# The down projections of a two-layer encoder: eleven Strassen pairs instead of ten pairs and two plain chunks, with the order of all queues written out

## The chip, the cores and the metric

One core of a Trainium2 chip runs the whole program in one launch. The metric is device time in microseconds (us) of one execution; less is better. The time before is the median of three runs.

## What is computed

The program is a bidirectional encoder trunk on 512 tokens of width 1024, two layers. Each layer has a half-step SwiGLU feed-forward block, an attention mixer, a second half-step feed-forward block and a gated per-layer input; a final RMSNorm closes it. All in float32. The part that matters here is the feed-forward block, run four times:

```python
def rmsnorm(x, g):
    y = xf * lax.rsqrt(jnp.mean(xf * xf, axis=-1, keepdims=True) + RMS_EPS)
    return (y * g.astype(jnp.float32)).astype(x.dtype)

def swiglu(x, w_gate, w_up, w_down):
    return (jax.nn.silu(x @ w_gate) * (x @ w_up)) @ w_down
...
for i in range(DEPTH):
    h = h + 0.5 * swiglu(rmsnorm(h, norm_ffn1[i]), ffn1_w_gate[i], ffn1_w_up[i], ffn1_w_down[i])
    ...
    h = h + 0.5 * swiglu(rmsnorm(h, norm_ffn2[i]), ffn2_w_gate[i], ffn2_w_up[i], ffn2_w_down[i])
    gate = jax.nn.sigmoid(rmsnorm(h, norm_ple[i]) @ w_ple_gate[i])
    h = h + gate * (p[i] @ w_ple_proj[i])
```

The inner width is 2816, that is 22 chunks of 128.

## The kernel before, in words

**Splitting.** Every float32 product is made of three TensorE matmuls on operands cut in two: a high part (ScalarE copies the value to the float32r type, L153) and a low part (VectorE subtracts the high part from the value, L154). `split` (L152) does both; `mm` runs high x high, high x low, low x high into the same PSUM bank. Weights come in tiles `wr` of 128x1024 (`WR` = 5 buffers) or `tmp` of 128x512 (`TMPS` = 10); their parts lie in `wh` and `wl` (4 buffers each).

**A feed-forward block** (`ffn`, L454). `front` and five calls of `block` make the gate and up products. Their rows are turned back by TensorE transposes (`turn_back`, L443: four transposes into a PSUM bank, then a ScalarE copy out at L450) into chunks `a[0..21]`, each 128 inner features x 512 tokens. `between` turns one block's rows while the next block runs; the last block's four chunks are turned inside the down stage, by the function `turn`. `inner_sums` (L492) makes three VectorE sums per pair of chunks, for pairs whose chunks are there (`READY`).

**The down stage** (`down`, L501) multiplies the chunks by the down weights. Two chunks (`WHOLE` = 2) are multiplied plainly: `rx`, then the halves `left` and `right`. The other 20 form `K2` = 10 pairs, each a 2x2 block product in Strassen's form (Winograd's variant), seven products of halves instead of eight. The functions `first` to `seventh` are these products; each takes a unit of two pairs, so there are five units. A product of one unit is 12 matmuls of 128x128 by 128x512: two pairs, two banks, three parts (L542 to L544).

The seven products need weights b11, b21, b22, b11 + b12 and so on. The sums of weights are made in the buffer itself: GpSimd issues a DMA that adds the next block to what lies there (`add`, L533) once the present weights have been split. `first` (L572) loads b11 (`load`, L517) and adds b12, which `fifth` uses; `summed` (L562) loads b12 and b22 and adds them on VectorE (L567), which `seventh` uses; adding b11 gives the weights of `sixth`, adding b21 those of `fourth`. `second` and `third` load b21 and b22 into `tmp` tiles through `halved` (L526).

**What sets the order.** The loops in `down` only state the work. The scheduler of the framework orders each engine's queue, by priorities in program order and its own estimate of when things are ready; buffers of the pools add the waits. Each engine runs its queue in that order and waits in place for what an instruction needs. SP's queue issues the loads, GpSimd's the adding loads. `tc.keep_in_program_order` (L150, in `put`) fixes the place of single instructions; before, only the setup uses it.

After the last product of a stage, the four output quarters are transposed (L677), added to the residual rows `hs`, which are loaded from DRAM (`kept`), and normed for the next stage, whose first matmuls are L178 to L180 or L803 to L805.

## Time and profile before

| | |
|---|---|
| median of 3 runs | 2003.8 us (2002.4 to 2007.15) |
| the profiled execution | 2005.77 us |
| its span, first to last instruction | 2003.9 us |
| mean granted TensorE clock | 0.997 |
| down stages in it, from the first to the last matmul | 230 to 343, 859 to 972, 1252 to 1364, 1817 to 1933 us |
| DMA over the span | 173 GB/s |

A row of the timeline has start, length, engine, line and operation, the tile written and those read, the shape, and in brackets the idle time before it and what ended it. PE is TensorE's matmul, PEld its weight load, DVE VectorE, ACT ScalarE, POOL GpSimd; a q behind the name is that engine's queue of issues. In a table of windows each engine's busy time stands with its number of instructions, and behind them the granted clock (1.00 is full), the share of the DMA engines and GB/s.

### The profile page before, as it was taken

The page shows a single profiled execution, that of the slowest core. Times are in us where ns is not written, and L with a number is a line of the kernel's source. Part 1 is how long each engine was busy: PE and PEld are TensorE (multiplying, and loading weights), DVE is VectorE, ACT ScalarE, POOL GpSimd, SP SyncE. Part 2 cuts the span into 40 slices and gives each one's busy share as a digit, 9 for nine tenths or more (in the row PEclk, how much of TensorE's full clock was granted, in tenths as well). Part 3 has the DMA queues.
Part 4 walks back from the last instruction along what each step waited for, and adds up shares of the span by engine and source line. Part 5 has one row for each costly group of instructions (what it writes and reads, how often), then busy time and mean ns, then how long its engine had stood idle before and what let it go on. Part 6 is the DMA issues. An engine that isn't in the chain of part 4 may idle for free.

```text
span 2003.9 us, 28013 instructions
## 1 busy us (share of the span) xinstructions
PE 1976.0 (99%) x9726; PEld 1646.1 (82%) x9726; DVE 1537.0 (77%) x2648; ACT 1213.0 (61%) x2051; POOL 324.7 (16%) x378
## 2 busy tenths in 40 slices
PE   9999999999999999999999999999999999999997
PEld 7888788879888888878888888788888888887886
DVE  7787897798767677797786778877888668778775
ACT  7656765477645565675566556745766556666553
POOL 1111011341211221111122110011000122110111
PEclk9999999999999999999999999999999999999999
DMA  9877687543426787878568786785343577776961
GB/s 274 196 198 174 170 213 225 141 95 78 96 73 221 173 184 173 195 188 222 189 214 186 178 190 168 209 212 162 104 129 100 188 181 188 176 173 177 230 222 43
DMA packets 151069, 346.12 MB, mean 173 GB/s; under 512 B 26384, under 2 KB 34064, under 8 KB 150928
## 3 DMA queue, kind: packets, MB, share of 16 engines
q1 hardware_dynamic: 112704, 236.28, 36.0%
q0 software_dynamic: 38080, 108.02, 30.5%
q8 instruction: 76, 1.25, 0.2%
q14 instruction: 65, 0.53, 0.1%
q10 hardware_dynamic: 144, 0.04, 0.0%
HBM read 315.96 MB, written 17.27 MB: 166 GB/s over the span
## 4 chain that ended last, share of the span: by engine, by line
PE 87%; DVE 5%; DMA 3%; issue 3%; ACT 2%; POOL 0%; DVEq 0%; ACTq 0%; POOLq 0%
PE mm L368 7%; PE mm L369 7%; PE mm L367 7%; PE mm L178 5%; PE mm L180 5%; PE mm L179 5%; PE sc L367 3%; PE sc L369 3%; PE sc L368 3%; PE mm L544 3%; PE mm L542 3%; PE mm L543 3%; PE sc L543 2%; PE sc L544 2%; PE sc L542 2%
## 5 line engine op out<-in xcount | busy, mean ns | idle before, releaser
L153 ACT ACTIVATE wh<-wr 128x1024 fp32r<-128x1024 f32 (+1 forms) x408 | 427.2, 1050 | 424.2 <-DMA wr<-in_gu_dram 82.3
L154 DVE TENSOR_TENSOR wl<-wr,wh 128x1024 fp32r<-128x1024 f32 (+1 forms) x408 | 496.2, 1219 | 199.5 <-ACT wh L153 197.0
L367 PE MATMUL mm<-wh,act 128*128 128x512 f32 x640 | 250.9, 392 | 0.0
L369 PE MATMUL mm<-wh,act 128*128 128x512 f32 x640 | 250.7, 392 | 0.0
L368 PE MATMUL mm<-wl,act 128*128 128x512 f32 x640 | 249.5, 390 | 0.6 <-DVE wl L154 0.5
L153 ACT ACTIVATE wh<-tmp 128x512 fp32r<-128x512 f32 x264 | 155.6, 625 | 95.8 <-PE sc L369 32.6
L178 PE MATMUL mm<-act,wh 128*128 128x512 f32 (+1 forms) x472 | 184.8, 393 | 0.4 <-ACT act L153 0.4
L179 PE MATMUL mm<-act,wh 128*128 128x512 f32 (+1 forms) x472 | 184.5, 391 | 0.0
L180 PE MATMUL mm<-act,wl 128*128 128x512 f32 (+1 forms) x472 | 184.4, 391 | 0.0
L154 DVE TENSOR_TENSOR wl<-tmp,wh 128x512 fp32r<-128x512 f32 x264 | 171.5, 683 | 4.1 <-ACT wh L153 3.7
L337 POOL DMA_DIRECT2D wr<-in_gu_dram x80 | 80.4, 1020 | 379.8 <-DVE wl L154 360.6
L368 PEld LDWEIGHTS mm<-wl,act 128*128 128x128 f32 x640 | 120.2, 188 | 25.7 <-DVE wl L154 1.5
L369 PEld LDWEIGHTS mm<-wh,act 128*128 128x128 f32 x640 | 120.2, 188 | 24.4
L367 PEld LDWEIGHTS mm<-wh,act 128*128 128x128 f32 x640 | 120.3, 188 | 23.8
L154 DVE TENSOR_TENSOR act<-act,act 128x512 fp32r<-128x512 f32 (+1 forms) x216 | 133.8, 634 | 3.8 <-ACT act L153 3.7
L153 ACT ACTIVATE act<-act 128x512 fp32r<-128x512 f32 (+1 forms) x216 | 120.7, 582 | 24.0 <-DVE act L311 9.9
L367 PE MATMUL sc<-wh,act 128*128 128x512 f32 x320 | 124.6, 389 | 1.6 <-DVE act L291 1.6
L369 PE MATMUL sc<-wh,act 128*128 128x512 f32 x320 | 124.7, 390 | 0.0
L368 PE MATMUL sc<-wl,act 128*128 128x512 f32 x320 | 124.5, 389 | 0.0
L409 DVE TENSOR_TENSOR wr<-wr,wr 128x1024 f32<-128x1024 f32 x40 | 49.0, 1225 | 87.8 <-DMA wr<-in_gu_dram 87.6
L533 POOL DMA_DIRECT2D wr<-in_dn_dram x60 | 51.9, 864 | 365.9 <-DVE wl L154 325.3
L345 POOL DMA_DIRECT2D tmp<-in_gu_dram x80 | 74.8, 1200 | 221.8 <-DVE act L498 137.0
(272 smaller groups left out, 4631.3 us busy)
## 6 DMA issues: line engine op xcount, KB each, us to landing
wr<-in_gu_dram SPq DMA_DIRECT2D x92, 512.0 KB, 5.2
tmp<-in_gu_dram SPq DMA_DIRECT2D x160, 256.0 KB, 3.7
wr<-in_gu_dram POOLq DMA_DIRECT2D x80, 512.0 KB, 7.6
tmp<-in_dn_dram SPq DMA_DIRECT2D x144, 256.0 KB, 4.0
wr<-in_dn_dram POOLq DMA_DIRECT2D x60, 512.0 KB, 6.3
tmp<-in_gu_dram POOLq DMA_DIRECT2D x80, 256.0 KB, 5.9
wr<-in_dn_dram SPq DMA_DIRECT2D x40, 512.0 KB, 4.4
act<-kept SPq DMA_DIRECT2D x56, 256.0 KB, 4.5
```

The lines of the kernel that those rows point to most:

```text
L153: self.put(self.nc.scalar.activation(hi, src, AF.Copy))
L154: self.put((lo_eng or self.nc.vector).tensor_tensor(lo, src, hi.bitcast(F32), op=ALU.subtract))
L178: mm(out, stat[0], mov[0], start=start, stop=False)
L179: mm(out, stat[0], mov[1], start=False, stop=False)
L180: return mm(out, stat[1], mov[0], start=False, stop=stop)
L337: nc.gpsimd.dma_start(raw, q[:, u * UNIT:(u + 1) * UNIT], accum_op=ALU.add)
L367: mm(p, xh, wh, start=start and k == 0, stop=False, skip_group_check=True)
L368: mm(p, xh, wl, start=False, stop=False, skip_group_check=True)
L369: self.last_mm = mm(p, xl, wh, start=False, stop=stop and k == half - 1, skip_group_check=True)
L542: mm(p, xh, wh, start=start and k == 0, stop=False, skip_group_check=True)
L543: mm(p, xh, wl, start=False, stop=False, skip_group_check=True)
L544: ins = mm(p, xl, wh, start=False, stop=stop and k == u.stop - 1, skip_group_check=True)
```

## The change

All 22 chunks now form pairs: `K2` = 11, `WHOLE` and all that served it are gone, and the weights are laid out in four quarters of eleven blocks (`_quarters`). The eleven pairs make six units, the first of one pair, the others of two. `READY` is 9, so that nine pairs have their inner sums before the stage.

A list `order` says in which order the 42 products run. Product by product, three functions are called: `product` (the matmuls), `after` (what follows certain products: transposes, copies out of banks, closing sums, loads of the residual) and `ahead`, which calls `prepare` (splits, sums, adding loads) for the product `LEAD` + 1 = 4 places on and `load` for the one 7 places on (3 and 6 before the first product runs). While `pinned` is set, `put` keeps all these instructions in program order on TensorE, VectorE, ScalarE, GpSimd and SP.

In a product the three parts now run one behind the other over the whole unit (high x high for both pairs and banks, then low operand x high weight, then high operand x low weight). The operand splits of the b halves are made as halves of 128x256 just ahead of `second` and `fourth`, not whole. The transposes of the last block's chunks use the `tr` banks, not the `sc` banks, and run in two groups, behind `first` of unit 2 and `fifth` of unit 1.

```diff
-WHOLE = 2
-READY = 8
-K2 = (NF - WHOLE) // 2
+READY = 9
+K2 = NF // 2
+LEAD = 3
+LOADS = 6
...
-                self.nc.tensor.transpose(p[:, b * P:(b + 1) * P], x[:, c * P:(c + 1) * P], self.ident)
-            self.nc.scalar.activation(a, p, AF.Copy)
+                self.put(self.nc.tensor.transpose(p[:, b * P:(b + 1) * P], x[:, c * P:(c + 1) * P], self.ident))
+            self.put(self.nc.scalar.activation(a, p, AF.Copy))
...
+        units = [range(1)] + [range(u, u + 2) for u in range(1, K2, 2)]
...
+        def half_split(x):
+            t = self.act(F32R)
+            self.split(x, t[:, l], t[:, r])
+            return t[:, l], t[:, r]
+
+        def inner_split(s):
+            for k in units[s]:
+                x3[k] = self.split_chunk(sums[k], nc.vector)
+                put(tt(B[k][:, l], B[k][:, l], sums[k][:, r], op=ALU.add))
...
+        def load(kind, s):
+            u = units[s]
+            if kind == "first":
+                raws[s] = wide(b11, u)
+            elif kind == "seventh":
+                raws[n + s], more[s] = wide(b12, u), narrow(b22, u)
+            elif kind in ("second", "third"):
+                more[kind, s] = narrow(b21 if kind == "second" else b22, u)
...
+        def prepare(kind, s):
+            u = units[s]
+            if kind == "first":
+                w = self.parts(raws[s])
+                add(raws[s], b12, u)
+                for k in u:
+                    if sums[k] is None:
+                        sums[k] = self.inner_sums(A[k], B[k])
+                    x1[k] = self.split_chunk(A[k], nc.vector)
+                x = x1
+            elif kind == "second":
+                w, x = halved(more.pop((kind, s))), {k: half_split(B[k][:, l]) for k in u}
+            elif kind == "fifth":
+                w, x = self.parts(raws.pop(s)), x1
+            elif kind == "seventh":
+                for j, y in enumerate(more.pop(s)):
+                    z = raws[n + s][:, j * T:(j + 1) * T]
+                    put(tt(z, z, y, op=ALU.add))
+                w, x = self.parts(raws[n + s]), x3
+                add(raws[n + s], b11, u)
+                if u.start not in x3:
+                    inner_split(s)
+            elif kind == "sixth":
+                w, x = self.parts(raws[n + s]), x3
+                add(raws[n + s], b21, u)
+            elif kind == "fourth":
+                for k in u:
+                    x2[k] = half_split(B[k][:, r])
+                w, x = self.parts(raws.pop(n + s)), x2
+            else:
+                for k in u:
+                    x4[k] = half_split(B[k][:, l])
+                w, x = halved(more.pop((kind, s))), x4
+            ops[kind, s] = w, x
+            if kind == "fifth" and 0 < s < 4:
+                inner_split(s - 1)
...
+            for a, b in ((0, 0), (1, 0), (0, 1)):
+                for j, k in enumerate(u):
+                    for i, p in enumerate(out):
+                        c = slice(cols.start + i * P, cols.start + (i + 1) * P)
+                        put(nc.tensor.matmul(p, x[k][a][:, c], w[b][:, j * T:(j + 1) * T], start=start and k == a == b == 0,
+                                             stop=stop and b == 1 and k == u.stop - 1, skip_group_check=True))
...
+        order = [(k, s) for s in range(n - 1) for k, s in (("second", s), ("first", s), ("fifth", s - 1)) if s >= 0]
+        order += [("seventh", 0), ("second", 5), ("first", 5), ("fifth", 4), ("seventh", 1), ("sixth", 0), ("seventh", 2),
...
+            elif (kind, s) == ("fourth", 0) and inner:
+                self.p = inner()
...
+        ahead(LEAD)
+        for i, step in enumerate(order):
+            product(*step)
+            if step == ("fourth", 5):
+                ahead(i + LEAD + 1)
+                after(*step)
+            else:
+                after(*step)
+                ahead(i + LEAD + 1)
```

The list goes on with seventh 2, fifth 5, sixth 1, seventh 3, fourth 0, sixth 2, third 0, seventh 4, fourth 1, sixth 3, seventh 5, fourth 2, sixth 4, fourth 3, sixth 5, fourth 4, third 1, fourth 5, and then third 2 to 5 (the number is the unit). The number of TensorE matmuls outside the down stages and their order do not change.

Three places show the moves. First VectorE's queue in the first down stage of the kernel before, where the first b12 + b22 sum (L567, tile `wr_530`) stands among operand splits (L154 writing `act`) and a weight split (L154 writing `wl`).

```order
L594 TENSOR_TENSOR act_253_1203<-act_253_1203,act_255_1213 128x256
L496 TENSOR_TENSOR act_466_2281<-act_466_2281,act_468_2288 128x256
L567 TENSOR_TENSOR wr_530_2533<-wr_530_2533,tmp_531_2535 128x512
L154 TENSOR_TENSOR act_475_2303<-act_313_1526,act_474_2302 128x512
L154 TENSOR_TENSOR wl_496_2384<-wr_490_2373,wh_495_2383 128x1024
L154 TENSOR_TENSOR act_477_2307<-act_317_1540,act_476_2306 128x512
```

Now the same sum (L566, tile `wr_501`) stands behind the splits of `first` and `fifth` of the units that run before it, directly ahead of the split of its own weights; its unit is the one of a single pair.

```order
L155 TENSOR_TENSOR act_506_2414<-act_380_1874,act_505_2413 128x512
L155 TENSOR_TENSOR act_508_2418<-act_384_1888,act_507_2417 128x512
L155 TENSOR_TENSOR wl_512_2438<-wr_463_2240,wh_511_2437 128x1024
L155 TENSOR_TENSOR act_514_2442<-act_255_1213,act_513_2441 128x512
L516 TENSOR_TENSOR act_250_1193<-act_250_1193,act_255_1213 128x256
L155 TENSOR_TENSOR act_516_2447<-act_256_1217,act_515_2446 128x512
L516 TENSOR_TENSOR act_254_1207<-act_254_1207,act_256_1217 128x256
L566 TENSOR_TENSOR wr_501_2392<-wr_501_2392,tmp_502_2394 128x512
L155 TENSOR_TENSOR wl_519_2467<-wr_501_2392,wh_518_2466 128x512
L155 TENSOR_TENSOR wl_521_2484<-tmp_509_2421,wh_520_2483 128x512
```

The sum has moved from the head of operand splits to their end. Second, SP's queue of loads before, around the load of that sum's weights (L517, `wr_530`); L566 are the b22 blocks of this and later sums, L526 weights of `second`.

```order
L526 DMA tmp_541_2570<-in_dn1_dram 128x512
L526 DMA tmp_542_2571<-in_dn1_dram 128x512
L566 DMA tmp_544_2592<-in_dn1_dram 128x512
L566 DMA tmp_545_2595<-in_dn1_dram 128x512
L517 DMA wr_530_2533<-in_dn1_dram 128x1024
L566 DMA tmp_553_2650<-in_dn1_dram 128x512
L566 DMA tmp_554_2653<-in_dn1_dram 128x512
```

Now the load (L520, `wr_501`) stands with its own b22 block (`tmp_502`) ahead of the loads of `second` (`tmp_509`, `tmp_510`) and `first` of unit 5 (`wr_517`).

```order
L520 DMA wr_480_2310<-in_dn1_dram 128x1024
L520 DMA wr_501_2392<-in_dn1_dram 128x512
L526 DMA tmp_502_2394<-in_dn1_dram 128x512
L526 DMA tmp_509_2421<-in_dn1_dram 128x512
L526 DMA tmp_510_2422<-in_dn1_dram 128x512
L520 DMA wr_517_2451<-in_dn1_dram 128x1024
L520 DMA wr_524_2495<-in_dn1_dram 128x1024
```

Each product's loads now stand together, in the order of the products. Third, VectorE's queue now, at the preparation of `seventh` of unit 4 in the same stage: two sums (L566), the low weight part, the two inner splits with their sums (L516), then the operands of `fourth` of unit 1.

```order
L566 TENSOR_TENSOR wr_567_2696<-wr_567_2696,tmp_568_2698 128x512
L566 TENSOR_TENSOR wr_567_2696<-wr_567_2696,tmp_569_2699 128x512
L155 TENSOR_TENSOR wl_578_2757<-wr_567_2696,wh_577_2756 128x1024
L155 TENSOR_TENSOR act_580_2762<-act_387_1901,act_579_2761 128x512
L516 TENSOR_TENSOR act_382_1881<-act_382_1881,act_387_1901 128x256
L155 TENSOR_TENSOR act_582_2767<-act_388_1905,act_581_2766 128x512
L516 TENSOR_TENSOR act_386_1895<-act_386_1895,act_388_1905 128x256
L155 TENSOR_TENSOR act_586_2783<-act_184_849,act_586_2783 128x256
```

Nothing of another product stands between the sums and the split that needs them.

More of the change, by code (lines that the diff above doesn't have):

```diff
@@ L409, in fifth @@
                 tt(base[i], base[i], chain[i], op=ALU.add)
-            late()
             product(A, base, t12, r, False, False)
@@ L499, in inner_sums, with down @@
         return s
-    def down(self, w, a, xs, x1, sums, begin, kept, inner, turn):
+    def down(self, w, a, sums, kept, inner, turn):
         nc, H = self.nc, T // 2
@@ new lines, in product @@
+        def product(kind, s):
+            u, (w, x) = units[s], ops.pop((kind, s))
+            out = {"first": r1, "second": r2, "fifth": r3, "seventh": rb, "sixth": r1, "fourth": rc, "third": r3}[kind]
+            cols = r if kind in ("fifth", "sixth") else l
+            start, stop = kind not in ("sixth", "third"), s == n - 1
+            for a, b in ((0, 0), (1, 0), (0, 1)):
[4 more added lines that the diff above has]
+                                             stop=stop and b == 1 and k == u.stop - 1, skip_group_check=True))
@@ L562, in summed @@
-        def summed(s):
-            raws[s] = load(b12, units[s])
-            for j, k in enumerate(units[s]):
-                x, more = raws[s][:, j * T:(j + 1) * T], self.tmp()
-                nc.sync.dma_start(more, b22[:, k * T:(k + 1) * T])
-                tt(x, x, more, op=ALU.add)
-        def first(s):
-            u = units[s]
-            raw = raws[s] = load(b11, u)
-            for k in u:
-                if sums[k] is None:
-                    with self.tc.issue_after(marks[s - 2].ins):
-                        sums[k] = self.inner_sums(A[k], B[k])
-                x1[k] = x1[k] or self.split_chunk(A[k], nc.vector)
-            marks.append(product(r1, u, self.parts(raw), x1, l, True, last(u)))
-            add(raw, b12, u)
@@ L598, in sixth @@
-        def sixth(s):
-            u = units[s]
-            product(r1, u, self.parts(raws[s]), x3, r, False, last(u))
-            add(raws[s], b21, u)
-        def fourth(s):
-            u = units[s]
-            product(rc, u, self.parts(raws[s]), x2, r, False, last(u))
-            for k in u:
-                t = self.act(F32R)
-                x4[k] = t[:, l], t[:, r]
-                self.split(B[k][:, l], *x4[k])
-        for s in range(n):
-            first(s)
-            if s == 1:
-                turn(range(2))
-            second(s)
-            if s == 1:
-                turn(range(2, 4))
-                r3 = [self.sbank(), self.sbank()]
-                c5 = copied(rx)
-            if s > 1:
-                fifth(s - 2)
@@ new lines, in down, with ahead @@
+        for i, step in enumerate(order[:LOADS]):
+            load(*step)
+            if i < LEAD:
+                prepare(*step)
+        self.pinned, end = True, len(order)
+        def ahead(i):
+            if i < end:
+                prepare(*order[i])
+            if i + LOADS - LEAD < end:
+                load(*order[i + LOADS - LEAD])
+        ahead(LEAD)
[4 more added lines that the diff above has]
+                after(*step)
+            else:
+                after(*step)
+                ahead(i + LEAD + 1)
```

191 lines of the change are left out of this document (67 added, 124 removed).

## The prediction

> **What bounds the kernel now.** I read the page first, then the waits of TensorE, then the timeline of the down stages.
>
> ```profile
> PE 1976.0 (99%) x9726; PEld 1646.1 (82%) x9726; DVE 1537.0 (77%) x2648; ACT 1213.0 (61%) x2051; POOL 324.7 (16%) x378
> PEclk9999999999999999999999999999999999999999
> ```
>
> TensorE is busy for 99% of the span at full granted clock, so time goes only by fewer matmuls or fewer gaps between them. The waits of TensorE (us in total, times, longest) name where it stands still:
>
> ```profile
> PE mm L544 <- DVE act L154: 4.7, 4, 2.1
> PE sc L449 <- ACT act L450: 3.2, 4, 0.8
> ```
>
> Both rows stand in the down stages, four times each, once per stage: 4.7 + 3.2 = 7.9 us.
>
> How fast it goes between gaps comes from the first down stage's timeline: its first matmul, two that bracket an undisturbed run, and its last.
>
> ```profile
> 230.03 0.39 PE L542 MATMUL tr<-wh,act 128*128 128x512 f32 x1
> ...
> 256.13 0.39 PE L542 MATMUL mm<-wh,act 128*128 128x512 f32 x1
> ...
> 272.22 0.39 PE L544 MATMUL sc<-wh,act 128*128 128x512 f32 x1
> ...
> 343.08 0.40 PE L544 MATMUL sc<-wh,act 128*128 128x512 f32 x1
> ```
>
> From 256.13 to 272.22 there are 71 starts: 16.09 / 71 = 0.2266 us a matmul. (The 0.39 is the pipelined length, not the pace.) How many there are, from the groups by line (L542 is one of the three matmuls of a split product, L543 and L544 have equal counts):
>
> ```profile
> L542 PE MATMUL mm<-wh,act 128*128 128x512 f32 x256 | 100.4, 392 | 0.0
> L542 PE MATMUL sc<-wh,act 128*128 128x512 f32 x176 | 69.3, 394 | 0.0
> L542 PE MATMUL ob<-wh,act 128*128 128x512 f32 x96 | 37.6, 392 | 0.0
> L542 PE MATMUL tr<-wh,act 128*128 128x512 f32 x96 | 37.4, 389 | 0.0
> ```
>
> 256 + 176 + 96 + 96 = 624, times 3 is 1872, 468 per down stage. First and last matmul of the other three stages:
>
> ```profile
> 859.12 0.39 PE L542 MATMUL tr<-wh,act 128*128 128x512 f32 x1
> ...
> 972.30 0.40 PE L544 MATMUL sc<-wh,act 128*128 128x512 f32 x1
> ...
> 1251.72 0.39 PE L542 MATMUL tr<-wh,act 128*128 128x512 f32 x1
> ...
> 1364.48 0.40 PE L544 MATMUL sc<-wh,act 128*128 128x512 f32 x1
> ...
> 1817.21 0.39 PE L542 MATMUL tr<-wh,act 128*128 128x512 f32 x1
> ...
> 1932.93 0.40 PE L544 MATMUL sc<-wh,act 128*128 128x512 f32 x1
> ```
>
> From first to last start the four stages take 113.05, 113.18, 112.76 and 115.72 us; 468 matmuls alone are 106.05. With the last matmul's own 0.23 the first stage has 113.28 - 106.05 = 7.2 us that are not matmuls; 40 transposes lie in it.
>
> **Where it stands still.** TensorE's rows around the two waits in the first stage:
>
> ```profile
> 240.91 1.04 PE L449 MATMUL sc<-ident,act 128*128 128x128 f32 x8
> ...
> 242.76 1.14 PE L449 MATMUL sc<-ident,act 128*128 128x128 f32 x8 [0.81 <-ACT act L450]
> ...
> 243.76 0.50 PE L542 MATMUL mm<-wh,act 128*128 128x512 f32 x1
> ...
> 248.18 0.39 PE L542 MATMUL sc<-wh,act 128*128 128x512 f32 x1
> ...
> 249.51 0.74 PE L544 MATMUL mm<-wh,act 128*128 128x512 f32 x2 [0.94 <-DVE act L154]
> ```
>
> The second group of eight transposes takes 1.00 us (242.76 to 243.76), 0.125 each; the first took 1.85, so 0.85 us went on waiting for ScalarE's copy out of the two banks. From 248.18 to 249.51 are 1.33 us instead of 0.23: 1.10 lost, waiting on VectorE for the low part of an operand. What VectorE was doing, and the load it waited for on SP's queue:
>
> ```profile
> 243.50 0.33 SPq L517 DMA_DIRECT2D wr<-in_dn_dram  x1
> ...
> 248.16 0.69 DVE L567 TENSOR_TENSOR wr<-wr,tmp 128x512 f32<-128x512 f32 x1 [2.12 <-DMA wr<-in_dn_dram]
> 248.77 0.69 DVE L154 TENSOR_TENSOR act<-act,act 128x512 fp32r<-128x512 f32 x1
> ```
>
> The load of the b12 weights was issued at 243.50. VectorE stood 2.12 us at the sum that needs it, and the operand split behind it in its queue (248.77) is the one TensorE wanted. So it is a load issued too late, met by an instruction queued too early. With transposes at 0.11 to 0.125 us each, 40 of them take 4.4 to 5.0 of the 7.2 us, so the stage's standstill, short restarts behind the waits among it, is 2.2 to 2.8 us; I take 2.3. In the fourth stage the same wait is longer, 2.11 us, and is followed by slow starts:
>
> ```profile
> 1837.87 0.73 PE L544 MATMUL mm<-wh,act 128*128 128x512 f32 x2 [2.11 <-DVE act L154]
> ...
> 1839.13 0.57 PE L543 MATMUL mm<-wl,act 128*128 128x512 f32 x1
> ...
> 1842.48 0.45 PE L544 MATMUL mm<-wh,act 128*128 128x512 f32 x1
> ```
>
> ```profile
> 1837.00:1841.00 4.00, 3.13 (x10) 2.50 (x11) 4.00 (x7) 0.00 (x0) 0.86 (x1) 0.77 0.33 76
> ```
>
> Between 1839.13 and 1842.48 eight matmuls take 3.35 us, not 1.81: 1.5 us more, at a mean granted clock of 0.77. The Trainium skill ("TensorE: Matmul & The Clock Gate", section "Why this matters for your kernels") asks only that idle gaps stay under about 3 us; by it this gap would have cost itself alone and the removable time would be 1.5 us less. Here a gap of 2.11 us was enough, so the measurement decides: a new wait above about 2 us is priced at itself plus 1.5.
>
> By the lengths of the stages (0.13 more, 0.29 less and 2.67 more than the first), the four lose 2.3 + 2.4 + 2.0 + 5.0 = 11.7 us; 13.7 with transposes at 0.11.
>
> **The change part by part.** *Eleven pairs by seven products.* Two of the 22 chunks went through the plain product: 2 chunks x 4 quarter products x 2 banks x 3 = 48 matmuls, beside 10 x 42 = 420. Now 11 x 42 = 462. Six fewer per stage, 24 in all, at 0.2266: 5.4 us, directly on TensorE's path, since nothing else is left to cover.
>
> *One written order.* The load of the first b12 unit now stands on SP's queue ahead of three products' worth of other loads, and the sum that needs it stands on VectorE's queue behind the operands of all products that run before it (the order rows above). That removes the wait for VectorE in every stage (4.7 us in the list) and the fourth stage's slow clock. The transposes of the last block now come in two groups with a product of 12 matmuls (2.7 us) between, which is longer than the wait of 0.85, so it goes too. Gone in the best case: all 11.7 us (13.7).
>
> *What is late next: VectorE.* Its load in the first down stage, in the order sum, TensorE, weight loads, VectorE, ScalarE, GpSimd:
>
> ```profile
> 230.00:361.00 131.00, 129.25 (x613) 107.06 (x612) 106.30 (x167) 77.49 (x121) 16.46 (x22) 1.00 0.80 214
> ```
>
> VectorE is at 106 of 131 us. The change adds to it per stage about 23 splits of 128x256 and one 128x512 weight split, one b12 sum and one set of pair sums, and takes ten 128x512 operand splits and two closing sums away. Its pace per operation by start-to-start distances, and one weight activation of ScalarE:
>
> ```profile
> 232.04 1.41 DVE L440 SCALAR_TENSOR_TENSOR act<-act,minus,act 128x512 f32<-128x512 f32 x2
> ...
> 236.91 0.68 DVE L154 TENSOR_TENSOR wl<-tmp,wh 128x512 fp32r<-128x512 f32 x1
> 237.51 1.22 DVE L154 TENSOR_TENSOR wl<-wr,wh 128x1024 fp32r<-128x1024 f32 x1
> 238.64 0.41 DVE L594 TENSOR_TENSOR act<-act,act 128x256 f32<-128x256 f32 x1
> ...
> 244.95 0.75 DVE L594 TENSOR_TENSOR act<-act,act 128x256 f32<-128x256 f32 x2
> ```
>
> ```profile
> 235.71 1.06 ACT L153 ACTIVATE wh<-wr 128x1024 fp32r<-128x1024 f32 x1 [0.52 <-ACT act L153]
> ```
>
> 128x512: 0.60 (236.91 to 237.51); 128x1024: 1.13 (237.51 to 238.64); 128x256: about 0.34 (a second one adds 0.33 to the 0.42 of a first). So 23 + 4 (of the sums) at 0.34, less 12 - 2 at 0.60: 9.2 - 6.0 = +3.2 us, about 109 of 129. On average it is covered. Locally, per product of 12 matmuls (2.72 us of TensorE): second and third 1.9 us, first 2.3, fifth and sixth 1.1, fourth 1.8, seventh 5.3 when it also splits its inner sums (two sums 1.2; then a standstill of 1.06 until ScalarE has made the high part; the low part 1.13; 2 x (0.60 + 0.34)). The four weight buffers let a product's preparation begin when the product three before it starts. For the seventh of unit 4 that is "fourth" of unit 0 (6 matmuls), "sixth" of 2 (12), "third" of 0 (6): 5.44 us against 5.3. For the seventh of unit 5: three products, 8.16 us, against 1.8 + 1.1 + 5.3 = 8.2. So both come in with nothing to spare; where the stage also splits two per-layer inputs (second and fourth stage), 1.2 us more falls into the second of these. In its favour, the new matmul order takes the high-by-high third first, so the operand's low part is wanted 0.9 us and the weight's 1.8 us after the product starts. At the start of a stage, VectorE's last two gate/up products (232.04, done at 233.45, 3.4 us into the stage) stand ahead of the two operand splits of the second "first" (1.2 us), so that these end at 4.6, while its turn comes after 6 + 6 + 12 matmuls, at 5.4: close, but early enough.
>
> I take 1.0 us per stage for all this, between 0 and the 2.1 us of the longest wait the trace has in these stages: 4 us in all, ends 0 and 8.4.
>
> *Loads.* Quarter blocks read per stage: 88 instead of 86 of 256 KB, +2.3%, no term. An accumulating load, issued by GpSimd when the first split of its buffer is done, lands as follows (median of issues by line; then min, median, max of L533):
>
> ```profile
> wr<-in_dn_dram POOLq DMA_DIRECT2D x60, 512.0 KB, 6.3
> ```
>
> ```profile
> DMA to landing us min/median/max: 5.3/6.3/9.3
> ```
>
> The closest users are now three products, 8.16 us, apart, as they were; at 6.3 us that is covered, at 9.3 not (third rival).
>
> *Tail, gate/up.* The end of a stage has the same transposes and evictions; one more set of pair sums in gate/up, 1.0 us of VectorE, lies under TensorE work. Zero for both; if the tail's cover is gone, a 1 us wait per stage, inside the range.
>
> **Sum.** 5.4 + 11.7 - 4.0 = 13.1 us. The profiled execution took 2005.8 us (span 2003.9, 1.9 around it), so 1992.7; the median of the three runs is 2.0 lower, 2003.8, so 1990.7, and I say 1990.5.
>
> **Rivals.** *Half the gain.* The sevenths' chain on VectorE costs 2 to 3 us a stage, since its two inner waits (sum, ScalarE, split) can no longer be filled by other work in a fixed order. For it: the margins of 0.1 us above, and a wait over 2 us brings the slow clock. Against it: low parts are wanted late. Gain 5.4 + 11.7 = 17.1 less 8 to 13: 4 to 9 us, 1995 to 1999.5.
>
> *Nothing.* Removed waits are replaced by equal ones: a gain within 4 us, 2000 to 2007.
>
> *Slower: the accumulating loads hold the fixed queues.* ScalarE already waits for them, by the waits of the first stage's window:
>
> ```profile
> ACT wh L153 <- DMA wr<-in_dn_dram: 19.3, 7, 4.2
> ```
>
> Seven waits, up to 4.2 us; now every later preparation stands behind such a wait. Place: seventh, sixth and fourth of unit 5, which hand one buffer on through two landings. The low weight part of that seventh is done 1.9 us before its product may start (the inner splits come behind it), and 7 products of 2.72 lie between the starts of seventh and fourth: 20.9 us for two landings and two splits of 1.06 + 1.13, so 8.2 us a landing. At the median 6.3 nothing waits. At 9.3, the maximum seen, 2.1 us are lost, with the slow clock 3.6 a stage, 14.4 of the 17.1 us of gain. At 10.5 it is 4.6 + 1.5 = 6.1 a stage, 24.4 in all, so 2003.8 + 7.3 = 2011. It decides from about 10 us on; only the maximum speaks for it. The Trainium skill (same page, Part 1) calls the queues of VectorE and ScalarE strictly first in, first out, which is the mechanism of this rival; the trace agrees (VectorE's 2.12 us at the b12 sum held the split behind it).
>
> That the order isn't what is written is excluded by the rows of the order.
>
> **Numbers.** Forecast (10 to 19 us gained) 0.6, half the gain 0.2, nothing 0.1, slower 0.1. The range reaches from 2003.8 - 5.4 - 13.7 = 1984.7, rounded down, to the top of the half gain, 1999.5, and leaves out the last two. About 0.2%, 4 us, is what a measurement of this kernel can tell from no change: faster 0.8, same 0.1, slower 0.1.
>
> **What would show it.** Right: 1848 matmuls of the down stages at 0.227 us; the waits on VectorE's low part and on ScalarE's copy in the list of TensorE's waits gone; stage lengths near 109 to 111 us each; no granted clock below 1 in the fourth. Half: TensorE waiting on VectorE or ScalarE ahead of a seventh or the product behind it. Slower: ScalarE waiting for accumulating loads with TensorE behind it, at the fourths and sixths of the last units. The prediction is wrong if the stages shrink by less than the 1.4 us that six matmuls are worth.

## The result and the profile after

The changed kernel takes 2024.27 us (median of four runs, 2023.78 to 2025.72), the kernel before beside it 2004.31: a ratio of 1.010 (95% interval 1.0082 to 1.0117), 20.0 us slower, where 13.3 us faster was forecast. The profiled execution took 2024.63 us, its span is 2022.8 us (+18.9) and its mean granted clock 0.992 (0.997 before). Medians here are of the runs at the usual clock: one run each of experiments 4 and 9, at a mean granted clock of 0.75 and 0.85, doesn't count.

The page after, and the waits of TensorE:

```profile
PE 1981.2 (98%) x9702; PEld 1649.2 (82%) x9702; DVE 1551.9 (77%) x2716; ACT 1217.7 (60%) x2107; POOL 335.2 (17%) x390
```

```profile
PE tr L614 <- DVE act L630: 12.5, 6, 3.0
PE mm L595 <- ACT wh L154: 9.3, 5, 5.3
```

The 24 matmuls are gone (9726 to 9702), and so are both old waits. Two new ones stand in their place, 21.8 us in all. L614 are the transposes of the tail, L630 the evictions of `second_half`, L595 the matmuls of the products, L154 ScalarE's high parts. First and last rows of the four stages, from the timeline of TensorE:

```profile
229.63 0.39 PE L595 MATMUL mm<-wh,act 128*128 128x512 f32 x1
...
347.02 1.08 PE L595 MATMUL sc<-wl,act 128*128 128x512 f32 x4
...
864.27 0.39 PE L595 MATMUL mm<-wh,act 128*128 128x512 f32 x1
...
986.25 1.07 PE L595 MATMUL sc<-wl,act 128*128 128x512 f32 x4
...
1266.18 0.39 PE L595 MATMUL mm<-wh,act 128*128 128x512 f32 x1
...
1379.32 1.08 PE L595 MATMUL sc<-wl,act 128*128 128x512 f32 x4
...
1831.87 0.39 PE L595 MATMUL mm<-wh,act 128*128 128x512 f32 x1
...
1951.66 1.08 PE L595 MATMUL sc<-wl,act 128*128 128x512 f32 x4
```

With three more starts in each last row (0.68 us), the stages take 118.1, 122.7, 113.8 and 120.5 us, 475.0 in all, against 454.7: +20.3 us. The rest of the program is 1.4 us shorter. All of the loss is in the down stages, most of it at two places.

**The tail, in every stage.** TensorE at the end of the first stage:

```profile
331.81 2.09 PE L595 MATMUL sc<-wh,act 128*128 128x512 f32 x8
333.74 1.08 PE L595 MATMUL sc<-wl,act 128*128 128x512 f32 x4
337.75 2.15 PE L614 MATMUL tr<-ident,act 128*128 128x128 f32 x8 [2.94 <-DVE act L630]
339.56 3.76 PE L595 MATMUL sc<-wh,act 128*128 128x512 f32 x8
343.12 1.34 PE L595 MATMUL sc<-wl,act 128*128 128x512 f32 x4
```

Behind third 3 eight transposes want the two `tr` banks, 2.94 us before VectorE has emptied them; the eight matmuls after it take 3.56 us (339.56 to 343.12), where those of third 3 took 1.93 (331.81 to 333.74). VectorE in the same stretch, and ScalarE's two rows that hold it up:

```profile
318.42 1.23 DVE L155 TENSOR_TENSOR wl<-wr,wh 128x1024 fp32r<-128x1024 f32 x1 [2.53 <-ACT wh L154]
...
324.62 1.23 DVE L155 TENSOR_TENSOR wl<-wr,wh 128x1024 fp32r<-128x1024 f32 x1 [2.44 <-ACT wh L154]
325.77 1.28 DVE L656 TENSOR_TENSOR act<-act,tr 128x512 f32<-128x512 f32 x2
...
328.17 0.75 DVE L155 TENSOR_TENSOR act<-act,act 128x256 fp32r<-128x256 f32 x2
...
334.47 1.28 DVE L155 TENSOR_TENSOR wl<-tmp,wh 128x512 fp32r<-128x512 f32 x2
335.67 0.68 DVE L662 TENSOR_TENSOR act<-mm,act 128x512 f32<-128x512 f32 x1
...
336.87 1.07 DVE L630 SCALAR_TENSOR_TENSOR act<-tr,act 128x256 f32<-128x256 f32 x3
```

```profile
317.32 1.06 ACT L154 ACTIVATE wh<-wr 128x1024 fp32r<-128x1024 f32 x1 [2.75 <-DMA wr<-in_dn_dram]
...
323.53 1.06 ACT L154 ACTIVATE wh<-wr 128x1024 fp32r<-128x1024 f32 x1 [2.88 <-DMA wr<-in_dn_dram]
```

ScalarE stands at the weights of fourth 4 and fourth 5 for their accumulating loads, VectorE behind it, 5 us in two pieces. From 325.77 on VectorE has no gap: closing sums, the preparations of four thirds (328.17 to 335.67), the sums for c21 (one of the four output quarters), and only then the evictions. By these rows it would be enough to be rid of about 3 of the 5 us, or of about 3 of the 7.5 us; experiments 6, 7 and 13 try both.

The kernel before stands still here too. In its first stage, VectorE's last wait of this kind, its first eviction, and the transposes that want the bank:

```profile
322.88 1.22 DVE L154 TENSOR_TENSOR wl<-wr,wh 128x1024 fp32r<-128x1024 f32 x1 [3.28 <-ACT wh L153]
...
335.20 0.74 DVE L693 SCALAR_TENSOR_TENSOR act<-tr,act 128x256 f32<-128x256 f32 x2
```

```profile
336.89 0.60 PE L677 MATMUL tr<-ident,act 128*128 128x128 f32 x4
```

From the end of the standstill to the first eviction it is about 12.3 us in both kernels. But counted from the stage's start the eviction comes 105.2 us in before and 107.2 after, and its transposes are wanted 106.9 us in before and already 105.2 after (2.94 us ahead of 337.75).

**Before fourth 1, in the second and fourth stage.** SP's issue of the per-layer inputs, ScalarE's splits of them, and TensorE:

```profile
922.66 0.97 SPq L481 DMA_DIRECT2D tmp<-in_pT_dram  x2
```

```profile
932.98 0.63 ACT L154 ACTIVATE act<-tmp 128x512 fp32r<-128x512 f32 x1 [5.58 <-DMA tmp<-in_pT_dram]
936.00 0.63 ACT L154 ACTIVATE act<-tmp 128x512 fp32r<-128x512 f32 x1 [2.40 <-DMA tmp<-in_pT_dram]
```

```profile
931.86 1.07 PE L595 MATMUL tr<-wl,act 128*128 128x512 f32 x4
938.24 0.79 PE L595 MATMUL mm<-wh,act 128*128 128x512 f32 x1 [5.31 <-ACT wh L154]
```

The loads land 10 and 13 us after their issue (in the fourth stage 9 and 10). The splits are fixed in ScalarE's queue, so the weights of fourth 1 stand behind them. The granted clock (third number from the right) behind the first stage's tail wait and behind this one:

```profile
338.00:345.00 7.00, 7.00 (x27) 5.60 (x27) 6.71 (x12) 5.29 (x9) 1.14 (x2) 0.60 0.44 152
937.00:946.00 9.00, 7.76 (x21) 6.11 (x22) 7.54 (x12) 6.18 (x10) 1.73 (x2) 0.62 0.56 160
```

### The profile page after: what moved, and what is told of

It reads as the page before. It is cut to its first block, busy times and chain, and to the rows that moved or that the text cites. A ratio compares the mean times of both kernels' runs of the same rounds, so it can differ in the third digit from the quotient of the medians.

```text
span 2022.8 us, 28037 instructions
## 1 busy us (share of the span) xinstructions
PE 1981.2 (98%) x9702; PEld 1649.2 (82%) x9702; DVE 1551.9 (77%) x2716; ACT 1217.7 (60%) x2107; POOL 335.2 (17%) x390
## 4 chain that ended last, share of the span: by engine, by line
PE 68%; DVE 4%; DMA 3%; ACT 2%; issue 2%; SPq 0%; POOL 0%; DVEq 0%; ACTq 0%; POOLq 0%
PE mm L369 5%; PE mm L370 5%; PE mm L368 5%; PE mm L179 5%; PE mm L595 5%; PE mm L181 5%; PE mm L180 5%; PE sc L595 3%; PE sc L370 3%; PE sc L368 3%; PE sc L369 3%; DMA wr<-in_dn_dram 2%; PE tr L449 2%; PE ob L595 1%; PE ob L368 1%
## 5 line engine op out<-in xcount | busy, mean ns | idle before, releaser
L154 ACT ACTIVATE wh<-wr 128x1024 fp32r<-128x1024 f32 (+1 forms) x428 | 438.0, 1029 | 441.0 <-PE mm L370 81.3
L155 DVE TENSOR_TENSOR wl<-wr,wh 128x1024 fp32r<-128x1024 f32 (+1 forms) x428 | 509.0, 1195 | 201.2 <-ACT wh L154 198.7
L368 PE MATMUL mm<-wh,act 128*128 128x512 f32 x640 | 250.7, 392 | 0.0
L370 PE MATMUL mm<-wh,act 128*128 128x512 f32 x640 | 250.6, 392 | 0.0
L154 ACT ACTIVATE wh<-tmp 128x512 fp32r<-128x512 f32 x248 | 145.2, 624 | 61.6 <-PE sc L370 32.4
L595 PE MATMUL mm<-wh,act 128*128 128x512 f32 x528 | 159.0, 395 | 9.3 <-ACT wh L154 9.3
L155 DVE TENSOR_TENSOR wl<-tmp,wh 128x512 fp32r<-128x512 f32 x248 | 160.4, 682 | 2.3 <-ACT wh L154 1.6
L155 DVE TENSOR_TENSOR act<-act,act 128x256 fp32r<-128x256 f32 (+1 forms) x268 | 140.8, 551 | 4.5 <-ACT act L154 4.3
L370 PEld LDWEIGHTS mm<-wh,act 128*128 128x128 f32 x640 | 120.1, 188 | 24.3
L368 PEld LDWEIGHTS mm<-wh,act 128*128 128x128 f32 x640 | 120.2, 188 | 23.7
L154 ACT ACTIVATE act<-act 128x256 fp32r<-128x256 f32 (+1 forms) x268 | 126.3, 514 | 16.3 <-DVE act L312 9.7
L595 PEld LDWEIGHTS mm<-wh,act 128*128 128x128 f32 x528 | 100.4, 190 | 32.3 <-ACT wh L154 11.4
L547 POOL DMA_DIRECT2D wr<-in_dn_dram x72 | 62.5, 882 | 362.3 <-DVE wl L155 359.5
```

Source lines behind the costliest of these rows:

```text
L154: self.put(self.nc.scalar.activation(hi, src, AF.Copy))
L155: self.put((lo_eng or self.nc.vector).tensor_tensor(lo, src, hi.bitcast(F32), op=ALU.subtract))
L368: mm(p, xh, wh, start=start and k == 0, stop=False, skip_group_check=True)
L370: self.last_mm = mm(p, xl, wh, start=False, stop=stop and k == half - 1, skip_group_check=True)
L547: put(nc.gpsimd.dma_start(raw, b[:, u.start * T:u.stop * T], accum_op=ALU.add))
L595: put(nc.tensor.matmul(p, x[k][a][:, c], w[b][:, j * T:(j + 1) * T], start=start and k == a == b == 0, stop=stop and b == 1 and k == u.sto ...
```

## Experiments

Theory: two separate losses, the late per-layer loads and the tail. Rivals: the accumulating loads are behind the tail; VectorE has too much work there; TensorE's transposes stand too early; the fixed order as a whole is too tight. Beside the groups of experiments (1 and 3 to 5; 6 and 8 to 10; 2, 7, 11 and 12; 13 and 14; 15 to 17) the kernel before had medians of 2004.8 to 2007.3 us, so 2 us between experiments of different groups tell nothing.

**1. Per-layer splits later.**

```diff
-        return self.split_chunk(raw, self.nc.vector)
+        return raw
...
             elif (kind, s) == ("fourth", 0) and inner:
-                self.p = inner()
+                raw = inner()
+            elif (kind, s) == ("seventh", 5) and inner:
+                self.p = [self.split_chunk(x, nc.vector) for x in raw]
```

> The changed kernel, with the splits of the two per-layer inputs moved from behind fourth 0 to behind seventh 5 in the written order (their loads stay where they are). Theory (the pinned splits wait for late loads and hold fourth 1's weights behind them): the waits of 5.3 and 2.2 us before fourth 1 in the second and fourth stage and the slow clock behind them go, 8.9 us in stage 2 and 5.0 in stage 4 (gaps of 5.47 and 3.35 us, plus 6.8 and 3.4 us at half clock), so 2024.3 - 13.9 = 2010.4; stage 2 shrinks from 122.0 to about 113, stage 4 from 119.8 to about 115, stages 1 and 3 stay at 117.4 and 113.6. Rival (accumulating loads hold the queues, or the order as a whole is too tight): the wait turns up at the next product, less than 4 us gained.

2006.84 us, 17.4 less than the changed kernel. The waits before fourth 1 are gone; stages 2 and 4 fall by 8.2 and 5.8 us. The first stage, which has no such inputs, fell by 3.8 as well: the waits before fourth 4 and fourth 5 are gone there, and the half clock behind its tail wait lasts 3.4 us instead of 6.8. Why they went is open. The median landing of its accumulating loads is 6.7 us instead of 7.8, but the two for fourth 4 and fourth 5 are no sooner there: from issue to ScalarE's start 8.0 and 8.1 us, against 8.4 and 8.0.

**2. Loads of the per-layer inputs earlier**, their splits in the old place.

```diff
-        return self.split_chunk(raw, self.nc.vector)
+        return raw
...
+            elif (kind, s) == ("sixth", 0) and inner:
+                raw = inner()
             elif (kind, s) == ("fourth", 0) and inner:
-                self.p = inner()
+                self.p = [self.split_chunk(x, nc.vector) for x in raw]
```

> The changed kernel with the loads of the per-layer inputs issued behind sixth 0, five products (12 us) earlier, and their splits fixed where the change has them, behind fourth 0. Theory (it is the late load, not the place or the length of the splits, that costs): the same as with the splits moved, 2005 to 2010. Rival (the 1.2 us of VectorE's work at that place is what costs): the wait before fourth 1 stays at 1 us or more and the gain under 8 us, 2016 or more.

2014.15 us, 10.1 less: between the two. The wait before fourth 1 is gone without moving the splits, so that wait was the load's. But 7.3 us of experiment 1's gain are missing: a few pieces of under 1 us stay in the second stage, one of 1.0 in the fourth, and all four tails wait 2.9 us. So the place of the splits costs something too.

**3. Evictions ahead of the last thirds in VectorE's queue.**

```diff
+                if x is c5:
+                    self.tc.keep_in_program_order(e)
...
-            if step == ("fourth", 5):
+            after(*step)
+            if i < end - LEAD - 3:
                 ahead(i + LEAD + 1)
-                after(*step)
-            else:
-                after(*step)
-                ahead(i + LEAD + 1)
+            elif step == ("third", 2):
+                ahead(end - 2)
+                ahead(end - 1)
```

> The changed kernel, with the evictions of the two second_half groups fixed in VectorE's queue ahead of the preparations of third 4 and third 5, which come behind third 2. Theory (in the tail TensorE's transposes wait for two banks whose evictions stand behind four thirds' preparations): the waits of L614 for L630 (about 3 us in each of the four stages) and the slow clock behind them (6.8, 3.4, 3.4 and 3.4 us at half rate) go, 12.1 + 8.5 = 20.6 us, so about 2004; since third 4 and 5 are now late by up to 1 us in some stages, up to 2008. Stage lengths near 110.5, 118, 109, 115. Rival (VectorE simply has too much to do in the tail): the wait moves to third 4 or third 5, and less than 6 us is gained.

2030.38 us, 6 us slower. TensorE at the first tail:

```profile
334.85 1.09 PE L614 MATMUL tr<-ident,act 128*128 128x128 f32 x4 [2.17 <-DVE act L630]
336.43 3.78 PE L595 MATMUL sc<-wh,act 128*128 128x512 f32 x8 [0.49 <-ACT wh L154]
```

The wait moves to the second half of that group and to third 4, at the same half clock: nothing is won by sorting a queue that is late as a whole.

**4. Edits 1 and 3 together.**

> Both edits together: the splits of the per-layer inputs behind seventh 5, and the tail's evictions ahead of the preparations of third 4 and 5. Theory: both losses go, 13.9 + 20.6 us, so 1990 (to 1994), below the kernel before by 10 to 14 us; all four stages at 109 to 111 us. Rival (accumulating loads): about 0.5 us remains at fourth 4 and fourth 5 of each stage in any case; if they are the true limit the two edits together save less than half of that sum.

2020.8 us, where 1990 to 1994 was expected. In sum the stages are no longer than in experiment 1, but matmuls of the next part now wait for VectorE:

```profile
PE mm L181 <- DVE wl L155: 5.3, 4, 2.4
```

**5. Nothing fixed in the down stages.**

```diff
-        self.pinned, end = True, len(order)
+        end = len(order)
...
                     first_half(2 * s - 5)
-                self.pinned = True
```

> The changed kernel with nothing fixed in its down stages: the same eleven pairs, the same written sequence of emission, but the scheduler places each instruction on its queue. Theory (the fixed queue order makes the losses, the pairs are a gain of 5.4 us): the long waits in the tail and before fourth 1 shrink, 1998 to 2010. Rival (the distribution of the pairs, or the lead of three products, is the cause): about 2024 as before, since the work emitted is the same.

2041.8 us, slower still, with other waits (14.0 us for low weight parts, up to 4.3). So fixing the queues is not the fault in itself: for this sequence the scheduler's order is worse.

**6. The thirds' operands split with the fourths**, on top of edit 1. The kernel before splits them there.

```diff
-                    x2[k] = half_split(B[k][:, r])
+                    x2[k], x4[k] = half_split(B[k][:, r]), half_split(B[k][:, l])
...
-                for k in u:
-                    x4[k] = half_split(B[k][:, l])
```

> The per-layer splits behind seventh 5 (as in the first experiment, 2006.8 us), and the thirds' operands split with the fourths, as the kernel before does it, where VectorE stands still 2.5 us each time for an accumulating load. Theory (in the tail VectorE is late by its own work): 4 x 0.67 us leave the tail's VectorE queue, the evictions end 2.7 us earlier, so TensorE's wait of 2.2 to 2.9 us for them falls below 0.5 us and the slow clock behind it (3.4 us at half rate, 1.7) goes: 4 x (2.7 + 1.7) = 17 us, so about 1990; at least 1996 if some of the clock loss stays. Rival (TensorE's fixed place for the transposes is what costs): the same, since this edit leaves them where they are, but then less than 8 us. Rival (accumulating loads set everything): 2003 to 2007.

1996.22 us, 10.6 less than edit 1 alone; the first stage is 3.7 us shorter (110.6) and no tail wait exceeds 0.5 us. Part of the stages' gain returns outside: between the first and second stage 521.3 us instead of 517.0, with two stretches of 3.4 us at half clock (from 387.4 and from 537.5) that experiment 1 doesn't have.

**7. The same edit alone on the changed kernel.**

> The changed kernel with one edit alone: the thirds' operands split with the fourths; the per-layer splits stay fixed behind fourth 0. Theory (two separate losses): this edit took 10.6 us off the kernel that had the per-layer splits moved (2006.8 to 1996.2), and should take the same off the changed kernel, 2024.3 to 2013.7 (2010 to 2016); the waits before fourth 1 (5.3 and 2.2 us) stay, those of the tail go. Rival (the two losses hang together, VectorE being late from one stage on): under 5 us, above 2019.

2005.49 us, 18.8 less, more than expected; the waits before fourth 1 stay:

```profile
PE mm L593 <- ACT wh L154: 8.6, 5, 4.0
```

The two gains apart are 17.4 + 18.8 = 36.2 us, together 28.1: they overlap, so two fully separate losses are not what the runs show.

**8. Transposes later**, on top of edit 1: in fours in the middle and at the end of third 4 and third 5.

```diff
+                    if kind == "third" and s > 3 and (a, j) == (1, 1):
+                        self.pinned = False
+                        first_half(2 * s - 8)
+                        self.pinned = True
...
-            if (kind, s) in (("fourth", 5), ("third", 2), ("third", 3), ("third", 4)):
+            if (kind, s) in (("fourth", 5), ("third", 2), ("third", 4), ("third", 5)):
...
-                    first_half(2 * s - 6)
-                    first_half(2 * s - 5)
+                    first_half(2 * s - 7)
```

> The per-layer splits behind seventh 5, and TensorE's first_half transposes one group of eight later and in fours: in the middle and at the end of third 4 and third 5, about where the kernel before has them, instead of eight behind third 3 and eight behind third 4. Theory (the transposes stand too early in TensorE's fixed queue): they are then wanted at 333.4 and 334.8 in the first stage instead of 331.9, the evictions they need are done at 334.9 and 335.9, so the wait falls from 2.9 to about 1.5 us and brings no slow clock: 4 x (1.4 + 1.7) = 12 us, so about 1995; if the next part of the program now starts late for want of the last norm splits, up to 2 us a stage come back, 2003. Rival (VectorE's backlog is the bound wherever the transposes stand): 2005 to 2010.

2001.87 us: 5.0 less. Waits of 0.9 to 1.6 us stay, at full clock.

**9. Edits 1, 6 and 8 together.**

> All three edits: per-layer splits behind seventh 5, thirds' operands split with the fourths, transposes in fours in and behind third 4 and 5. Theory: no wait above 0.5 us is left in the tails, stage lengths 109 to 110.5, 1987 to 1991, below the kernel before by 15 us. Rival (what is gained in the tail is lost at the start of the next part, which needs the norm splits of the chunks that are now transposed later): 1996 to 2004, with waits of matmuls of the next part on VectorE or ScalarE.

1994.9 us, no better than 1 and 6 (six runs, 1993.0 to 2003.2): the tail has no wait left, 0.5 to 1.2 us remain before fourths and in the next part.

**10. The kernel before with its tail's matmuls and transposes fixed**, in groups of eight.

```diff
-            mm = nc.tensor.matmul
+            mm = lambda *a, **k: kept_order(nc.tensor.matmul(*a, **k)) if tail else nc.tensor.matmul(*a, **k)
...
+                if tail:
+                    kept_order(t)
```

> The kernel before, with one thing of the change put in: in the tail TensorE's matmuls of the thirds and its transposes are fixed in the written order, so that the transposes stand in groups of eight behind third 2 and third 3 instead of where the scheduler put them in the middle of the thirds. Theory (the fixed place of the transposes costs the tail, since the evictions of the two banks come no earlier): a wait of 2 to 3 us per stage and 1.7 us of slow clock, 4 x 4 = 16 us, so about 2020. Rival (only VectorE's extra work of the thirds' operand splits makes the wait): under 4 us, 2004 to 2009.

2011.53 us, a ratio of 1.0021 (1.0009 to 1.0033): about 5 us, a third of what was expected. The grouping costs little by itself.

**11. That kernel with the thirds' operands split at the thirds.**

> The kernel before with the tail of the change put in: its thirds' products and its transposes fixed in the written order (that alone gave 2011.5), and the operands of its thirds split at the thirds instead of behind the fourths. Theory (VectorE's late work in the tail, met by transposes that can't move): 4 x 0.67 us more of VectorE ahead of the evictions, so waits of 2 to 3 us and a slow clock per stage as in the changed kernel's tails, 2011.5 + 10 = about 2021 (2016 to 2024). Rival (the tail is late because the fixed fourths wait for accumulating loads): no more than 2 us beside 2011.5.

2063.07 us, but not by the wait in question:

```profile
PE sc L536 <- ACT act L153: 20.3, 9, 3.2
```

The thirds wait for their own operand splits, which without a written lead come just in time or too late. This run tells nothing of the tail.

**12. More time for the accumulating loads**: edits 1, 6 and 8, and two thirds moved forward.

```diff
-                  ("fourth", 4), ("third", 1), ("fourth", 5)] + [("third", s) for s in range(2, n)]
+                  ("third", 1), ("fourth", 4), ("third", 2), ("fourth", 5)] + [("third", s) for s in range(3, n)]
...
-                elif s == 2:
+                elif s == 3:
                     second_half(M + 2, c5, r)
```

> All three edits (per-layer splits later, thirds' operands with the fourths, transposes in fours in and behind third 4 and third 5), and third 1 and third 2 moved ahead of fourth 4 and fourth 5, so that an accumulating load has four products (10.9 us) to land instead of three; the second group of evicted halves comes behind third 3. Theory (what is left of waits in the stages, 0.5 to 1.2 us before fourth 4 and fourth 5, is the accumulating loads): these waits go, 2 to 3 us less than 1997, 1993 to 1995. Rival (no cover is left for the transposes, with only three thirds behind fourth 5): a wait in the tail again, 1999 or more.

1987.42 us (1986.21 to 1990.09), a ratio to the kernel before of 0.9913 (0.9899 to 0.9928): the fastest kernel that leaves nothing out, 17.4 us below the kernel before and 36.9 below the changed one. 7.5 us less than experiment 9, where 2 to 3 were expected. Its first stage:

```profile
229.33 0.39 PE L597 MATMUL mm<-wh,act 128*128 128x512 f32 x1
...
337.34 1.09 PE L597 MATMUL sc<-wl,act 128*128 128x512 f32 x4
```

That is 108.7 us, and TensorE has no wait above 0.2 us from 295 to 345.

**13. Accumulating loads of the last two units left out**, on top of edit 1 alone.

```diff
-                add(raws[n + s], b11, u)
+                if s < 4:
+                    add(raws[n + s], b11, u)
...
-                add(raws[n + s], b21, u)
+                if s < 4:
+                    add(raws[n + s], b21, u)
```

> The kernel with the per-layer splits behind seventh 5 (2006.8 us), leaving out the accumulating loads of the last two units behind seventh and sixth (four of 512 KB per down stage), so that the weights of those sixths and fourths are not the reference's; everything else, the splits of the thirds in the tail among it, stays. If the tail is late because the fixed queues stand still for these loads (third rival), ScalarE's waits of 2 to 2.9 us before the last fourths go, VectorE comes about 5 us earlier to the thirds, and TensorE's waits of 2.2 to 2.9 us for the evictions go with their slow clock: 1988 to 1994. If VectorE's own work in the tail makes it late (four thirds' preparations can't be started before their weight buffers come free), the waits stay above 1.5 us, 2000 to 2006.

The weights of those sixths and fourths are then not the right ones. 1988.06 us, 18.8 less than with them. VectorE in its first stage:

```profile
317.49 1.28 DVE L660 TENSOR_TENSOR act<-act,tr 128x512 f32<-128x512 f32 x2 [1.47 <-ACT act L603]
...
327.40 0.68 DVE L666 TENSOR_TENSOR act<-mm,act 128x512 f32<-128x512 f32 x1
...
328.60 1.07 DVE L632 SCALAR_TENSOR_TENSOR act<-tr,act 128x256 f32<-128x256 f32 x3
```

The thirds' splits, the order of VectorE's queue and the place of the transposes are those of experiment 1; the evictions come at 328.60 instead of 334.06, and no tail waits for them. Busy times from 308 to 326 us (TensorE, weight loads, VectorE, ScalarE), here and in experiment 1:

```profile
308.00:326.00 18.00, 18.00 (x83) 14.89 (x83) 16.36 (x30) 13.81 (x30) 0.00 (x0) 1.00 0.64 244
```

```profile
308.00:326.00 18.00, 17.84 (x81) 14.55 (x81) 11.08 (x18) 10.29 (x23) 0.86 (x1) 1.00 1.05 340
```

VectorE does 16.4 us of work in this stretch instead of 11.1. So the prediction's third rival holds: without the standstill for these loads the same work comes in time. With the standstill left in, 2.7 us less work ahead of the evictions (6 and 7) helped as well, so the wait needs both. (The edit also takes 8 MB of loads away; that the lighter traffic helps as well is not excluded.)

**14. The same loads left out, with edits 1, 6 and 8.**

> The kernel with all three edits (1997.0 us), leaving out the same four accumulating loads per down stage. If what moving third 1 and third 2 forward gained (1997.0 to 1987.4) is the waits for these loads, this kernel comes to the same, 1986 to 1990, and TensorE's waits of 0.5 to 1.2 us before fourth 4 and fourth 5 go. If it was the other place of the thirds in the tail, 1993 or more.

1988.45 us, the same as 12 and 13: what moving the thirds gained is the waits for these loads.

**15 and 16. Loads of the residual later**, with edit 1 and alone.

```diff
-            elif (kind, s) == ("fourth", 2):
+            elif (kind, s) == ("third", 1):
                 hs.extend(self.act() for _ in range(KC))
                 for m in range(KC):
-                    nc.sync.dma_start(hs[m], kept[m])
+                    put(nc.sync.dma_start(hs[m], kept[m]))
```

> The kernel with the per-layer splits behind seventh 5 (2006.8 us), with the loads of the eight residual chunks issued behind third 1 in SP's order instead of behind fourth 2, so at about 320 us and later in the first stage instead of 297 to 301. If contention with these 2 MB makes the accumulating loads late, ScalarE's waits of 2 to 2.9 us before the last fourths shrink below 1.5 us, VectorE is early enough in the tail, and TensorE's waits for the evictions go: 1988 to 1996. If three products are too short for these loads anyhow, 2002 to 2007. If the residual chunks now come too late, VectorE waits for them at the evictions, up to 3 us a stage, 2007 to 2020.

> The changed kernel with only the residual loads moved behind third 1. If contention with them is behind the tail's loss, the tails' 12.1 us of waits and most of their slow clock go, and the waits before fourth 1 in the second and fourth stage stay: 2024.3 - 16 = 2008 (2004 to 2012). If not, 2018 or more.

2017.35 and 2024.85 us. SP now issues the residual at 322.7 us in the first stage, and VectorE waits for it ahead of the evictions:

```profile
DVE act L630 <- DMA act<-in_xT_dram: 2.5, 1, 2.5
```

With edit 1, ScalarE still waits for the first stage's accumulating loads, up to 3.5 us (2.9 in experiment 1). Their median landing is 7.2 us (6.7 in experiment 1); without edit 1 it is 6.0 us (7.8 in the changed kernel). So these two runs don't tell whether this traffic slows the loads; what does stays open.

**17. The same move in the kernel of 12.**

> The kernel with all three edits and thirds 1 and 2 moved forward (1987.4 us), with the residual loads moved behind third 1 as well. It has no wait of over 0.4 us left in its down stages, so there is nothing more to gain: 1986 to 1989 if the residual chunks come in time, and up to 2 us a stage more, 1995, if they don't.

1989.27 us: as expected, nothing more.

## Why the prediction was wrong

**Fewer matmuls, and the waits removed: right.** 24 matmuls and both old waits are gone. Where the new losses are taken away, the first stage has 108.7 us (113.05 before), a little under the 109 to 111 forecast, and the kernel 1987.4 us where 1990.5 was said for the change as a whole. Its four stages take 434.8 us, 19.9 less than before; 5.4 are the matmuls, so the removable standstill was 14.5 us, more than the 11.7 taken.

**Stalls at the sevenths, 4 us: too dear.** No gap above 0.35 us stands at a seventh in any stage.

**Loads, "no term": the step that failed first.** The median over the whole run, 6.3 us, was set against 8.16. In the first stage alone the changed kernel's trace gives

```profile
DMA to landing us min/median/max: 4.1/7.8/9.2
```

and GpSimd's issues of the two loads that matter, for fourth 4 and fourth 5, are

```profile
308.93 0.87 POOL L547 DMA_DIRECT2D wr<-in_dn_dram  x1 [3.95 <-DVE wl L155]
315.51 0.87 POOL L547 DMA_DIRECT2D wr<-in_dn_dram  x1 [5.71 <-DVE wl L155]
```

From there to ScalarE's 317.32 and 323.53 are 8.4 and 8.0 us, at the limit of 8.2 worked out in the third rival.

**Tail, "zero": failed.** "The same transposes and evictions" was true, but not their cover: VectorE comes late from 5 us of standstill, and 4 x 0.67 us of the thirds' operand splits, which the kernel before makes behind the fourths, have moved in ahead of the evictions. The price named for lost cover, 1 us a stage, is measured at 2.9 to 3.1 from start to start.

**The per-layer inputs, "1.2 us more": failed.** Only VectorE's splits were counted. Their loads weren't followed; they come 9 to 13 us after issue, and with the splits fixed the waits are 5.3 and 2.2 us.

**The slow clock: right in kind, a little small.** It was priced at 1.5 us behind a wait above 2 us, and the sum had no such wait. The mean clock fell from 0.997 to 0.992, worth 10 us (2 us either way for rounding), behind six waits, so 1.7 each. With the gaps of 0.25 us and more in the four stages, from start to start and less the pace, 12.3 in the tails, 7.8 before fourth 1, 2.3 before fourth 4 and 5 and 2.2 between transposes, the sum is 24.5 + 10 - 17.1 = 17.4 of the 20.3 us; 3 are left to smaller gaps and to the rounding.

**The third rival** named the mechanism and the place (fixed queues held by accumulating loads at the last fourths), with a chance of 0.1 and "from about 10 us on". It priced only what reaches TensorE directly, which was 0.6 us twice in the first stage. That ScalarE's standstill hands itself to VectorE, and VectorE's to the evictions 10 us later, was left out; so it decided from about 8 us.

## What to carry to other kernels

In a queue fixed by hand a standstill isn't lost at the place where it happens but at the next place without slack: follow each late load through every engine behind it to the end of the stage. Compare a load's distance with the landings of its own stretch, not with the run's median, and when a step is moved, follow its loads too. If a queue is late as a whole, give it more time (other products ahead of the wait) rather than another order at its end.

## What the runs showed of the hardware

Behind a wait of TensorE above about 2 us the clock was mostly halved, but these traces show no sharp limit. In experiment 5 TensorE waited 1.68 us before 326.01, and the clock stayed full; in experiment 3 it waited 2.17 us before 334.85, and ran at half for 6 us:

```profile
326.00:332.00 6.00, 5.99 (x26) 4.97 (x27) 4.36 (x6) 4.04 (x8) 0.00 (x0) 1.00 0.53 143
```

```profile
334.80:341.00 6.20, 5.66 (x15) 4.33 (x16) 5.72 (x12) 6.20 (x13) 0.58 (x1) 0.50 0.12 45
```

Between and even beyond these two the length alone doesn't decide. In experiment 5, a wait of 1.74 us before 1958.46 was followed by a granted clock of 0.72 over 6 us, one of 1.75 us before 1385.96 by 1.00. In experiment 11 the clock stayed full behind 3.19 us:

```profile
978.24 0.50 PE L536 MATMUL sc<-wh,act 128*128 128x512 f32 x1 [3.19 <-ACT act L153]
```

```profile
978.00:985.00 7.00, 4.35 (x19) 2.96 (x19) 4.24 (x10) 2.96 (x7) 0.00 (x0) 1.00 0.06 8
```

The Trainium skill ("TensorE: Matmul & The Clock Gate", section "Why this matters for your kernels") asks for no idle gap above about 3 us. These traces don't agree: 2.2 us were enough here, and 2.1 in the prediction's row of the kernel before.
